# Modulation parts of a two-layer trunk: other places in the program, and another way of ordering them

## The chip, the cores and the metric

The kernel runs on one core of one Trainium2 chip. The metric is the device time of one execution in microseconds (us), median of the runs. Engines are named as in the profile: PE is TensorE's matmul row, PEld its weight loads, DVE VectorE, ACT ScalarE, POOL GpSimd, SP SyncE; a name with q (ACTq, SPq) is that engine's sequencer, here issuing DMAs.

## What is computed

One inference step of a trunk with two layers, for 512 latent tokens and 128 context tokens (640 columns together), model width 1024, all float32:

```python
def trunk_layer(x, cond, l, P, rope, ctx):
    mod = (jax.nn.silu(cond) @ P['w_mod'][l] + P['b_mod'][l])[:, None, :]
    sh1, sc1, g1, sh2, sc2, g2 = jnp.split(mod, 6, axis=-1)
    h = rmsnorm(x) * (1.0 + sc1) + sh1
    mix, ctx_out = token_mixer(h, l, P, rope, ctx)
    x = x + g1 * mix
    h = rmsnorm(x) * (1.0 + sc2) + sh2
    u = dwconv3(h @ P['w_up'][l], P['ffn_conv_w'][l], P['ffn_conv_b'][l])
    x = x + g2 * ((jax.nn.silu(u[..., :D_FF]) * u[..., D_FF:]) @ P['w_down'][l])
    return x, ctx_out
```

`token_mixer` projects h once and feeds three branches (spatial gating, a two-directional mLSTM, differential attention); each is projected by `w_branch`, multiplied by a sigmoid gate, summed, and multiplied by `w_out`. The condition vectors do not depend on the layer's input, so a layer's modulation can be computed at any time before its first use.

## The kernel before

Features lie on the 128 partitions, tokens along the free axis. A product in full precision is three passes (high x high, high x low, low x high), two matmuls of 320 columns each, so a tile of 128 outputs from 1024 inputs is 48 matmuls, and a branch tile from 512 inputs 24. These are called bulk products here: all go through `mm` (L132) or `tm` (L160). `weights` loads 512 KB through SP's queue into `raw` (3 buffers), ACT casts it to `whi`, DVE or POOL subtracts to `wlo`, 512 columns at a time (4 buffers of each).

Order of a layer: `spatial`, `mlstm_in`, four times (`mlstm_qk`, `mlstm_head`, two tiles of the first branch), `attn_v`, four times (`attn_qk`, `attn_head`, with `mlstm_out` and the second branch between them), five gates ahead, `attn_out`, the last branch over eight tiles m, `w_out`, `ffn`. The FFN runs in three groups: up products f, then down products m over the eight output tiles. The instructions are traced in program order, and a planner with a time model of its own sets the final order on every engine at build time: a ready instruction with the earlier place goes first, heads have high priority, and an instruction under `keep_in_program_order` stays behind the one traced before it on its engine.

The modulation of a layer is 12 parts (six sections of 1024, two halves of 512 each). A part needs eight DMAs of 256 KB from `w_mod`, eight float32 products of 32 x 512 (L279; the trace has 16 matmuls for them), a copy out of PSUM (`modev`, L284), four transposes (L292) and two small DVE operations (L296, L300 or L302). Sections 0 and 1 of layer 0 are made in `start`. All others are 512 wide: `mod_load` loads a part, `mod_turn` closes the open part (transposes), sums the part that was loaded, and loads the next through ACT's queue; `mod_step` does one part at once. A part occupies a PSUM tile of the tag "ms" (two buffers, also used by the heads) from its products to its close.

In the kernel before, layer 0 makes six parts and layer 1 five from `mod_step` to the last branch: one in the buffers "y", one loaded ahead into "wk", then one turn behind each tile m of the last branch, all with the same eight "wk" buffers. The FFN of layer 0 makes seven more (the rest of its own and the first five of layer 1), that of layer 1 two. With `pin` the products and the transposes keep program order.

Of the kernel before, what the change touches and what calls it, by code (L numbers as in the profile page):

```python
# [51 lines left out]

T_MLQ, T_MLG, T_SGU, T_DAQ, T_MLO, T_GATE = 0, 8, 9, 13, 21, 25
G_SG, G_ML, G_DA = 2, 1, 0


class Tags:
# [9 lines left out]
class Trunk:  # L67
    def __init__(self, nc, tc, ins, outs, depth):
        self.nc, self.tc, self.I, self.O, self.L = nc, tc, ins, outs, depth
        self.n = 0  # L70
        self.flip = 0

        self.mod_held = self.mod_open = None
        self.behind = False

    def t(self, pool, shape, dt, tag, bufs=None):
        self.n += 1
# [42 lines left out]
    def mm(self, acc, w, k0, xs, halves=(0, 1), ks=None, pin=False):  # L120

        nc = self.nc
        last = len(xs) - 1
        for k in range(len(xs)) if ks is None else ks:
            hi, lo = w[(k0 + k) // 4]
            sl = slice((k0 + k) % 4 * P, ((k0 + k) % 4 + 1) * P)
            xh, xl = xs[k]
            terms = ((hi, xh), (hi, xl), (lo, xh))
            for i, (a, b) in enumerate(terms):
                for s in halves:  # L130
                    s = slice(s * NHALF, (s + 1) * NHALF)
                    ins = nc.tensor.matmul(acc[:, s], a[:, sl], b[:, s], start=k == 0 and i == 0,  # L132
                                           stop=k == last and i == 2)
                    if pin or self.behind:
                        self.tc.keep_in_program_order(ins)
                        self.behind = False

    def fm(self, l, tile_idx, xs):
        acc = self.psA()
# [1 line left out]
        self.mm(acc, w, 0, xs)  # L141
        return acc

    def tm(self, l, kind, xs, evac):


        nc = self.nc
        for nh in range(2):
            ps = [self.t(self.ps, [P, 1024], F32, "acc", 2), self.psM()]
            accs = [ps[b // 4][:, b % 4 * 256 : b % 4 * 256 + 256] for b in range(NB)]  # L150
            for kh in range(2):
                for i, (hi, lo) in enumerate(self.weights(self.I["w_in_v"][l, kind, nh, kh], 4 * 256)):
                    for b in range(NB):
                        bs = slice(b * P, (b + 1) * P)
                        for k in range(2):
                            xh, xl = xs[4 * kh + 2 * i + k]
                            sl = slice(k * 256, (k + 1) * 256)
                            for j, (a, w) in enumerate(((xh, hi), (xh, lo), (xl, hi))):
                                first, last = kh + i + k + j == 0, kh + i + k + j == 5
                                nc.tensor.matmul(accs[b], a[:, bs], w[:, sl], start=first and b % 2 == 0,  # L160
                                                 stop=last and (b % 2 == 1 or b == NB - 1))
            for b in range(NB):
                evac(b, nh, accs[b])

# [82 lines left out]
        self.lam = self.t(lp, [P, 1], F32, "lam", 2)  # L247
        nc.vector.tensor_scalar(self.lam, s[:, 0:1], s[:, 1:2], self.lam_init, ALU.subtract, ALU.add)

    def mod_part(self, l, sec, c0, width, src, pin=False):  # L250

        self.mod_vector(*self.mod_products(l, sec, c0, width, src, pin))

    def mod_products(self, l, sec, c0, width, src, pin=False):
        return self.mod_sums(l, sec, c0, width, src, self.mod_weights(l, sec, c0, width, src), pin)

    def mod_weights(self, l, sec, c0, width, src, eng=None):
# [14 lines left out]
    def mod_sums(self, l, sec, c0, width, src, raws, pin):  # L272

        nc = self.nc
        pool, tag, per = src
        ps = self.psM()
        for k in range(KD):
            j = 32 * (k % 4)
            ins = nc.tensor.matmul(ps[j : j + 32, 0:width], self.cs[:, k, :], raws[k], start=k < 4, stop=k >= 4,  # L279
                                   tile_position=(0, j))  # L280
            if pin:
                self.tc.keep_in_program_order(ins)
        ev = self.t(pool, [P, width], F32, "ev") if width < 512 else self.t(self.sp, [P, width], F32, "modev", 1)
        (nc.scalar.copy if pin else nc.vector.tensor_copy)(ev, ps[:, 0:width])  # L284
        return l, sec, c0, width, ps, ev, pin

    def mod_vector(self, l, sec, c0, width, ps, ev, pin):
# [13 lines left out]
        else:  # L301
            nc.vector.tensor_add(m, m, b)  # L302

    def mod_step(self, src, pin=False):
        if self.mod_todo:
            l, sec, n = self.mod_todo.pop(0)
            self.mod_part(l, sec, 512 * n, 512, src, pin)

    def mod_load(self, src, eng=None):

        if self.mod_todo:
# [4 lines left out]
    def mod_turn(self, src):  # L316

        self.mod_close()
        if self.mod_held:
            self.mod_open = self.mod_sums(*self.mod_held, True)  # L320
            self.mod_held = None
            self.behind = True

        self.mod_load(src, self.nc.scalar)

# [469 lines left out]
        return ys  # L795


    def attn_v(self, l, h):
# [10 lines left out]
        self.tm(l, 2, h, evac)  # L809
        return v  # L810

    def attn_qk(self, l, h, head):

        nc, p = self.nc, self.p1
        qk = []
        for i in range(2):
            acc = self.fm(l, T_DAQ + H * i + head, h)
            x = self.t(p, [P, NT], F32, "qk")
            nc.scalar.copy(x, acc)
# [102 lines left out]
    def branch(self, l, n, h, ys, merged, ms, first=False, last=False, ahead=None):  # L922
# [4 lines left out]
        for m in ms:  # L927
# [9 lines left out]
                nc.gpsimd.tensor_add(merged[m], merged[m], th)  # L937
            if last:
                out.append(self.split(merged[m], self.hp, "h", scale=0.5))
                self.mod_turn((p, "wk", 1))  # L940
        if last:
            self.mod_close()
        return out


    def ffn(self, l, h, accs, x, p2, nxt):
# [28 lines left out]
        for f0, f1 in FFN_PARTS:  # L975

            for f in range(len(acts), min(f1 + 1, NF)):
                up(f)
                if f in (2, 4):
                    self.mod_turn((p2, "mw", 1))  # L980
            g2 = self.mods[l, 5]
            down = lambda m: self.I["w_down"][l, m, :, f0 * P : f1 * P]
# [16 lines left out]
    def run(self):  # L999
# [3 lines left out]
        with ExitStack() as ctx:  # L1003
# [15 lines left out]
            for l in range(self.L):  # L1019
# [4 lines left out]
                self.layer_consts(l)  # L1024
                with tc.tile_pool(name=f"p1{l}", bufs=1, reuse_waits="tile") as p1:
                    self.p1 = Tags(p1, {"wk": 8, "tg": 2, "st": 6, "qk": 4, "v": 1, "y": 8, "hs": 5, "mg": 8})
                    merged = [self.t(self.p1, [P, NT], F32, "mg") for _ in range(KD)]
                    self.mod_todo = [(l, s, n) for s in (2, 3, 4) for n in range(2)][1 if l else 0 :]
                    ys = self.spatial(l, h, accs)
                    v, rows = self.mlstm_in(l, h)  # L1030
                    sums = self.t(self.sp, [P, H, NB], F32, "mlsum", 1)
                    hs = []
                    for i in range(H):
                        q, k = self.mlstm_qk(l, h, i)
                        if i == 0:
                            rows = (*rows[:2], self.gate_columns(rows[2]))
                        with tc.high_priority():
                            hs.append(self.mlstm_head(l, i, q, k, v, rows, sums))
                        self.branch(l, G_SG, h, ys, merged, (2 * i, 2 * i + 1), first=True)
                    self.lambdas(l)  # L1040
                    v = self.attn_v(l, h)
                    dsums = self.t(self.sp, [P, H, NB], F32, "dasum", 1)
                    os = []
                    for i in range(H):
                        q, k = self.attn_qk(l, h, i)
                        with tc.high_priority():
                            os.append(self.attn_head(l, i, q, k, v, dsums))
                        if i == 0:
                            ys = self.mlstm_out(l, h, hs, sums)
                        else:  # L1050
                            self.branch(l, G_ML, h, ys, merged, range(*FILL_ML[i - 1 : i + 1]))
                    ahead = {m: self.gate(l, G_DA, m, h, t) for m, t in enumerate(AHEAD)}
                    self.mod_step((self.p1, "y", 1), pin=True)
                    self.mod_load((self.p1, "wk", 1))
                    ys = self.attn_out(os, dsums)
                    mix = self.branch(l, G_DA, h, ys, merged, range(KD), last=True, ahead=ahead)
                with tc.tile_pool(name=f"p2{l}", bufs=1, reuse_waits="tile") as p2:
# [12 lines left out]
                    h2, accs = self.handoff([I["w_out"][l, m] for m in (KD - 2, KD - 1)], mix, x, self.mods[l, 2], st,  # L1070
                                            [I["w_up"][l, i] for i in range(2)])
                    nxt = l + 1 < self.L
                    self.mod_todo = [(l, 5, 0), (l, 5, 1)]
                    if nxt:
                        self.mod_todo += [(l + 1, s, n) for s in (0, 1) for n in range(2)] + [(l + 1, 2, 0)]
                    h, accs = self.ffn(l, h2, accs, x, tags, nxt)
                    if nxt:
                        for k in range(KD):
# [104 lines left out]
```

## Time and profile before

| | |
|---|---|
| median of 3 runs | 2437.73 us (2436.23 to 2439.9) |
| profiled execution, its time | 2434.44 us |
| its span in the profile | 2432.6 us |
| PE busy, PEld busy | 2391.6 us (98%), 2314.6 us (95%) |
| DVE, ACT, POOL busy | 1137.4, 949.9, 668.5 us |
| granted TensorE clock, mean | 0.997 |
| DMA | 227.39 MB, mean 93 GB/s |

The span runs from the first to the last instruction; the execution's own time has 1.8 us around it. The end of a matmul is modelled in these records, and matmuls overlap, so a stretch with a busy PE may still hold waits: the start-to-start distance of the products and the PEld column show them.

### The profile page before, as it was taken

What the parts mean: (1) busy time and instruction counts of PE and PEld (TensorE: products, weight loads), DVE (VectorE), ACT (ScalarE), POOL (GpSimd) and SP (SyncE); (2) the same over time, 40 slices, a digit from 0 to 9 for tenths busy, and PEclk for the clock granted to TensorE, in tenths of its full rate; (3) what the DMA queues carried; (4) which work ended last, traced back from release to release, by engine and by line L of the source; (5) the groups of instructions that cost most, each with busy time, mean ns of one, the idle gap of its engine ahead of it and who ended that gap; (6) DMA issues with size and microseconds to landing.
All of it is one profiled execution on the core that took longest, in us unless ns stands there. A gap on an engine that the chain in (4) does not pass through costs nothing.

```text
span 2432.6 us, 40611 instructions
## 1 busy us (share of the span) xinstructions
PE 2391.6 (98%) x16708; PEld 2314.6 (95%) x16708; DVE 1137.4 (47%) x2102; ACT 949.9 (39%) x1737; POOL 668.5 (27%) x486
## 2 busy tenths in 40 slices
PE   8999999999999999999999999999999999999998
PEld 7999999999699999999999999999987999999998
DVE  5455546554246423424446455455533454343344
ACT  4433335545145323323454332454542443232334
POOL 2312232332222322323213222323322223232231
PEclk9999999999999999999999999999999999999999
DMA  7222221124541444222322212211233432222222
GB/s 278 70 79 66 66 78 54 63 76 135 170 151 64 137 138 139 73 75 79 97 87 70 72 64 68 71 58 63 83 126 123 148 104 66 83 70 79 79 70 70
DMA packets 88761, 227.39 MB, mean 93 GB/s; under 512 B 9472, under 2 KB 23936, under 8 KB 88576
## 3 DMA queue, kind: packets, MB, share of 16 engines
q1 hardware_dynamic: 72448, 195.43, 24.5%
q10 hardware_dynamic: 16128, 29.37, 3.6%
q8 instruction: 131, 2.15, 0.4%
q14 instruction: 54, 0.44, 0.1%
HBM read 217.41 MB, written 7.35 MB: 92 GB/s over the span
## 4 chain that ended last, share of the span: by engine, by line
PE 93%; DVE 3%; DMA 2%; ACT 1%; issue 1%; ACTq 0%; SPq 0%; DVEq 0%; POOL 0%; POOLq 0%
PE acc L132 76%; PE acc L160 6%; PE ms L906 2%; PE ms L877 2%; PE ms L279 2%; PE ms L160 1%; DMA wk<-w_mod 1%; PE ms L899 1%; PE ms L753 1%; PE ms L742 1%; PE ms L755 1%; DVE h L393 1%; DVE x L476 0%; DVE wlo L104 0%; PE ms L707 0%
## 5 line engine op out<-in xcount | busy, mean ns | idle before, releaser
L132 PE MATMUL acc<-h,whi 128*128 128x320 f32 x6464 | 1243.5, 310 | 9.8 <-DVE h L393 5.0
L132 PEld LDWEIGHTS acc<-h,whi 128*128 128x128 f32 x6464 | 1019.2, 188 | 21.5 <-DVE h L393 9.3
L103 ACT CAST whi<-raw 128x512 fp32r<-128x512 f32 x596 | 365.2, 614 | 998.4 <-PE acc L132 725.9
L132 PE MATMUL acc<-h,wlo 128*128 128x320 f32 x3232 | 754.9, 309 | 0.0
L104 POOL TENSOR_TENSOR wlo<-raw,whi 128x512 fp32r<-128x512 f32 (+1 forms) x298 | 390.8, 1312 | 1320.4 <-ACT whi L103 1299.3
L132 PEld LDWEIGHTS acc<-h,wlo 128*128 128x128 f32 x3232 | 544.2, 188 | 0.2
L104 DVE TENSOR_TENSOR wlo<-raw,whi 128x512 fp32r<-128x512 f32 (+1 forms) x298 | 240.4, 807 | 457.8 <-ACT whi L103 438.0
L132 PE MATMUL acc<-act,whi 128*128 128x320 f32 x1408 | 268.9, 310 | 0.0
L132 PEld LDWEIGHTS acc<-act,whi 128*128 128x128 f32 x1408 | 221.9, 188 | 3.4 <-issue 3.4
L132 PE MATMUL acc<-act,wlo 128*128 128x320 f32 x704 | 165.6, 309 | 0.0
L536 DVE SCALAR_TENSOR_TENSOR x<-acc,mod,x 128x128 f32<-128x128 f32 (+3 forms) x136 | 66.3, 526 | 193.9 <-PE acc L132 193.9
L132 PE MATMUL acc<-y,whi 128*128 128x320 f32 x768 | 151.5, 312 | 1.7 <-DVE y L117 1.7
L160 PE MATMUL acc<-whi,h 128*128 128x256 f32 x768 | 145.7, 283 | 0.0
L169 DVE SCALAR_TENSOR_TENSOR cw<-acc,vec,cw 128x511 f32<-128x511 f32 (+1 forms) x176 | 95.7, 544 | 105.1 <-ACT cw L167 103.7
L132 PEld LDWEIGHTS acc<-y,whi 128*128 128x128 f32 x768 | 121.0, 188 | 8.9 <-issue 5.0
L160 PEld LDWEIGHTS acc<-whi,h 128*128 128x128 f32 x768 | 123.0, 192 | 0.0
L132 PEld LDWEIGHTS acc<-act,wlo 128*128 128x128 f32 x704 | 119.0, 188 | 0.0
L954 POOL TENSOR_TENSOR cw<-cw,cw 128x640 f32<-128x640 f32 x44 | 69.4, 1576 | 156.4 <-DVE cw L171 152.9
L160 PE MATMUL acc<-wlo,h 128*128 128x256 f32 x384 | 108.7, 283 | 0.0
L171 DVE SCALAR_TENSOR_TENSOR cw<-acc,vec,cw 128x511 f32<-128x511 f32 (+1 forms) x176 | 96.7, 550 | 6.1
L132 PE MATMUL acc<-y,wlo 128*128 128x320 f32 x384 | 90.6, 313 | 0.0
L885 ACT ACTIVATE wk<-ms,mx 128x640 f32<-128x640 f32 (+1 forms) x80 | 56.7, 709 | 76.6 <-DVE mx L883 73.1
(256 smaller groups left out, 2418.6 us busy)
## 6 DMA issues: line engine op xcount, KB each, us to landing
raw<-w_in_f SPq DMA_DIRECT2D x98, 512.0 KB, 3.3
raw<-w_up SPq DMA_DIRECT2D x88, 512.0 KB, 3.3
wk<-w_mod ACTq DMA_DIRECT2D x56, 256.0 KB, 5.1
mw<-w_mod ACTq DMA_DIRECT2D x56, 256.0 KB, 5.4
raw<-w_down SPq DMA_DIRECT2D x32, 448.0 KB, 3.3
raw<-w_in_v SPq DMA_DIRECT2D x24, 512.0 KB, 3.5
raw<-w_branch SPq DMA_DIRECT2D x24, 512.0 KB, 3.4
mw<-w_mod SPq DMA_DIRECT2D x16, 512.0 KB, 8.7
```

The costliest lines, as they stand in the source:

```text
L103: nc.scalar.copy(hi, raw[:, a:b])
L104: self.alt().tensor_sub(lo, raw[:, a:b], hi.bitcast(F32))
L132: ins = nc.tensor.matmul(acc[:, s], a[:, sl], b[:, s], start=k == 0 and i == 0, stop=k == last and i == 2)
L160: nc.tensor.matmul(accs[b], a[:, bs], w[:, sl], start=first and b % 2 == 0, stop=last and (b % 2 == 1 or b == NB - 1))
L169: nc.vector.scalar_tensor_tensor(dst[:, a + 1 : b], acc[:, a : b - 1], w0, dst[:, a + 1 : b], ALU.mult, ALU.add)
L171: nc.vector.scalar_tensor_tensor(dst[:, a : b - 1], acc[:, a + 1 : b], w2, dst[:, a : b - 1], ALU.mult, ALU.add)
L279: ins = nc.tensor.matmul(ps[j : j + 32, 0:width], self.cs[:, k, :], raws[k], start=k < 4, stop=k >= 4, tile_position=(0, j))
L536: self.nc.vector.scalar_tensor_tensor(x[:, a:b], acc[:, a:b], g[:, k, i : i + 1], x[:, a:b], ALU.mult, ALU.add)
L877: nc.tensor.matmul(ps[:, s : s + 320], st[:, qs], kk[:, s : s + 320], start=i == 0, stop=i == 1)
L885: nc.scalar.activation(e[:, 0:nk], ps[:, 0:nk], AF.Exp, bias=mx, scale=scale, accum_out=sm[:, j : j + 1])
L906: nc.tensor.matmul(po, at[:, c * P : (c + 1) * P], vv, start=c == 0, stop=c == n - 1)
L954: nc.gpsimd.tensor_mul(cs[0], cs[0], cs[1])
```

## The change

Four things. (1) The parts made around the last branch are gone: `mod_step`, the load into "wk" and the turns in `branch`. (2) Layer 0 makes its six parts earlier in the mixers: three in the buffers "mg" (the sums of the branches, not yet allocated then), after `spatial`, after `mlstm_in` and after the first `mlstm_qk`; three in the buffers "y" between the first branch's end and the use of the same tag by `mlstm_out`: in the middle of `attn_v`, after it, and between the two products of the first `attn_qk`. (3) Layer 1 makes none: the FFN of layer 0 makes 14 parts (its own last two and all twelve of layer 1), with a turn at every even f in place of 2 and 4; the FFN of layer 1 has none left. (4) A part is no longer pinned: its first product is ordered behind the last bulk matmul traced, each product behind the one before, and the next bulk matmul behind the last product; these are orders on PE's queue and no waits. The transposes are free for the planner. The copy out of PSUM is always on ACT.

```diff
@@ class Trunk
-        self.behind = False
+        self.behind = self.bulk = None
@@ mm
-                    if pin or self.behind:
-                        self.tc.keep_in_program_order(ins)
-                        self.behind = False
+                    self.queue(ins, pin)
+
+    def after(self, ins, prev):
+        self.tc.add_manual_dep(ins.ins, prev.ins.name, ORDER, reason="queued in this order")
+
+    def queue(self, ins, pin=False):
+        if pin:
+            self.tc.keep_in_program_order(ins)
+        if self.behind:
+            self.after(ins, self.behind)
+            self.behind = None
+        self.bulk = ins
@@ tm
+            if nh and between:
+                between()
@@ mod_sums
             if pin:
                 self.tc.keep_in_program_order(ins)
+            elif k:
+                self.after(ins, prev)
+            elif self.bulk:
+                self.after(ins, self.bulk)
+            prev = ins
+        if not pin:
+            self.behind = ins
@@ mod_turn
-            self.mod_open = self.mod_sums(*self.mod_held, True)
+            self.mod_open = self.mod_sums(*self.mod_held, False)
             self.mod_held = None
-            self.behind = True
@@ attn_qk
         for i in range(2):
+            if i and turn:
+                self.mod_turn(None)
             acc = self.fm(l, T_DAQ + H * i + head, h)
@@ branch
-                self.mod_turn((p, "wk", 1))
-        if last:
-            self.mod_close()
@@ ffn
-                if f in (2, 4):
+                if f % 2 == 0:
                     self.mod_turn((p2, "mw", 1))
@@ run
-                    merged = [self.t(self.p1, [P, NT], F32, "mg") for _ in range(KD)]
-                    self.mod_todo = [(l, s, n) for s in (2, 3, 4) for n in range(2)][1 if l else 0 :]
+                    self.mod_todo = [] if l else [(l, s, n) for s in (2, 3, 4) for n in range(2)]
+                    room = (self.p1, "mg", 1)
+                    self.mod_load(room)
                     ys = self.spatial(l, h, accs)
+                    self.mod_turn(room)
                     v, rows = self.mlstm_in(l, h)
+                    self.mod_turn(room)
...
                         if i == 0:
+                            todo, self.mod_todo = self.mod_todo, []
+                            self.mod_turn(None)
+                            self.mod_todo = todo
+                            merged = [self.t(self.p1, [P, NT], F32, "mg") for _ in range(KD)]
                             rows = (*rows[:2], self.gate_columns(rows[2]))
...
+                        self.mod_close()
+                    room = (self.p1, "y", 1)
+                    self.mod_load(room)
                     self.lambdas(l)
-                    v = self.attn_v(l, h)
+                    v = self.attn_v(l, h, lambda: self.mod_turn(room))
+                    self.mod_turn(room)
...
                         if i == 0:
+                            self.mod_close()
                             ys = self.mlstm_out(l, h, hs, sums)
...
-                    self.mod_step((self.p1, "y", 1), pin=True)
-                    self.mod_load((self.p1, "wk", 1))
...
-                    self.mod_todo = [(l, 5, 0), (l, 5, 1)]
                     if nxt:
-                        self.mod_todo += [(l + 1, s, n) for s in (0, 1) for n in range(2)] + [(l + 1, 2, 0)]
+                        self.mod_todo = [(l, 5, 0), (l, 5, 1)] + [(l + 1, s, n) for s in range(6) for n in range(2)]
```

## Rows read from the trace of the kernel before

**Rows 1.** The page: span, busy time of each engine, chain's shares by engine.

```profile
span 2432.6 us, 40611 instructions
PE 2391.6 (98%) x16708; PEld 2314.6 (95%) x16708; DVE 1137.4 (47%) x2102; ACT 949.9 (39%) x1737; POOL 668.5 (27%) x486
PE 93%; DVE 3%; DMA 2%; ACT 1%; issue 1%; ACTq 0%; SPq 0%; DVEq 0%; POOL 0%; POOLq 0%
```

**Rows 2.** Windows: stretch, busy per engine (instructions), PE clock, DMA share, GB/s.

```profile
135.00:311.00 176.00, 176.00 (x1259) 175.61 (x1258) 89.70 (x169) 54.35 (x86) 41.26 (x31) 1.00 0.21 67
606.00:655.00 49.00, 45.84 (x221) 24.44 (x221) 13.41 (x17) 6.67 (x11) 11.37 (x8) 1.00 0.58 193
1810.00:1853.00 43.00, 39.81 (x206) 23.60 (x206) 11.88 (x16) 6.24 (x10) 9.05 (x7) 1.00 0.51 171
883.00:898.00 15.00, 15.00 (x112) 13.19 (x104) 3.38 (x10) 2.85 (x5) 2.60 (x2) 1.00 0.63 202
```

**Rows 3.** Waits of PE's weight loads: waiter, releaser, total us, times, longest.

```profile
PEld ms L279 <- DMA wk<-w_mod: 32.0, 45, 2.1
```

**Rows 4.** Chain of waits, layer 0's last branch: start us, us, what.

```profile
591.73 8.21 PE acc L132 x56
599.93 1.98 PE ms L279 x16
...
606.86 3.79 PE acc L132 x24
...
654.47 10.76 PE acc L132 x72
665.23 0.44 PE ms L292 x4
```

**Rows 5.** Chain of waits, layer 1's last branch.

```profile
1803.96 1.98 PE ms L279 x16
...
1810.88 3.78 PE acc L132 x24
...
1852.08 0.44 PE ms L292 x4
```

**Rows 6.** Chain of waits in the mixers of layer 0.

```profile
135.19 14.09 PE acc L132 x96
...
341.72 17.62 PE acc L132 x120
```

**Rows 7.** Chain of waits in the FFN of layer 0.

```profile
765.77 28.39 PE acc L132 x192
794.16 1.85 PE ms L279 x16
...
883.71 12.52 PE acc L132 x84
...
926.27 1.98 PE ms L279 x16
...
928.97 0.66 PE ms L292 x4
```

**Rows 8.** Timeline of ACT in layer 0's last branch: start, us, engine, line, operation.

```profile
623.17 0.59 ACT L284 COPY modev<-ms 128x512 f32<-128x512 f32 x1 [5.38 <-PE ms L279]
623.25 3.71 ACTq L265 DMA_DIRECT2D wk<-w_mod  x8
...
633.72 0.59 ACT L284 COPY modev<-ms 128x512 f32<-128x512 f32 x1 [6.04 <-PE ms L279]
```

**Rows 9.** Timeline of all engines where the first mixer begins.

```profile
40.68 10.77 SPq L97 DMA_DIRECT2D raw<-w_in_v  x4
...
48.30 1.12 ACT L103 CAST whi<-raw 128x512 fp32r<-128x512 f32 x2
...
51.85 0.28 PE L160 MATMUL ms<-whi,h 128*128 128x256 f32 x1
```

**Rows 10.** Timeline of DVE in the first mLSTM head.

```profile
162.91 0.82 DVE L722 TENSOR_TENSOR st<-ms,wk 128x640 f32<-128x640 f32 x1
```

More of the change, by code (lines that the diff above doesn't have):

```diff
@@ L54 @@
 G_SG, G_ML, G_DA = 2, 1, 0
+ORDER = mybir.DependencyInfo(mybir.DependencyClass.NoSync, mybir.DependencyReason.DATA)
 class Tags:
@@ L142, in fm, with tm @@
         return acc
-    def tm(self, l, kind, xs, evac):
+    def tm(self, l, kind, xs, evac, between=None):
         nc = self.nc
         for nh in range(2):
+            if nh and between:
+                between()
             ps = [self.t(self.ps, [P, 1024], F32, "acc", 2), self.psM()]
@@ L159, in tm @@
                                 first, last = kh + i + k + j == 0, kh + i + k + j == 5
-                                nc.tensor.matmul(accs[b], a[:, bs], w[:, sl], start=first and b % 2 == 0,
-                                                 stop=last and (b % 2 == 1 or b == NB - 1))
+                                self.queue(nc.tensor.matmul(accs[b], a[:, bs], w[:, sl], start=first and b % 2 == 0,
+                                                            stop=last and (b % 2 == 1 or b == NB - 1)))
             for b in range(NB):
@@ L248, in lambdas @@
         nc.vector.tensor_scalar(self.lam, s[:, 0:1], s[:, 1:2], self.lam_init, ALU.subtract, ALU.add)
-    def mod_part(self, l, sec, c0, width, src, pin=False):
-        self.mod_vector(*self.mod_products(l, sec, c0, width, src, pin))
     def mod_products(self, l, sec, c0, width, src, pin=False):
@@ L282, in mod_sums @@
                 self.tc.keep_in_program_order(ins)
+            elif k:
[5 more added lines that the diff above has]
+            self.behind = ins
         ev = self.t(pool, [P, width], F32, "ev") if width < 512 else self.t(self.sp, [P, width], F32, "modev", 1)
-        (nc.scalar.copy if pin else nc.vector.tensor_copy)(ev, ps[:, 0:width])
+        nc.scalar.copy(ev, ps[:, 0:width])
         return l, sec, c0, width, ps, ev, pin
@@ L302, in mod_vector @@
             nc.vector.tensor_add(m, m, b)
[L304 to L307, printed above, removed]
     def mod_load(self, src, eng=None):
@@ L795, in mlstm_out, with attn_v @@
         return ys
-    def attn_v(self, l, h):
+    def attn_v(self, l, h, turn):
         nc, p = self.nc, self.p1
@@ L807, in evac, with attn_qk @@
                 nc.sync.dma_start(self.O["nv"][l, :, nh * 256 : (nh + 1) * 256], v[b][:, nh * 256 : (nh + 1) * 256])
-        self.tm(l, 2, h, evac)
+        self.tm(l, 2, h, evac, turn)
         return v
-    def attn_qk(self, l, h, head):
+    def attn_qk(self, l, h, head, turn):
         nc, p = self.nc, self.p1
@@ L1044, in run @@
                     for i in range(H):
-                        q, k = self.attn_qk(l, h, i)
+                        q, k = self.attn_qk(l, h, i, i == 0)
                         with tc.high_priority():
```

## The prediction

> **What bounds the kernel now.** I read the page first: PE is busy for 98% of the span, its weight loads for 95%, and 93% of the chain that ended last is PE [rows 1]. So a change that keeps the number of products, as this one does, can gain only where PE stands still. The busy share hides such places, because the end of a matmul is modelled; the PEld column of the windows shows them. In the mixers it fills the stretch (175.61 of 176 us), in the last branch of either layer it fills about half (24.44 of 49 us, 23.60 of 43 us) [rows 2]. The waits name the cause: PE's weight loads wait 32.0 us for w_mod transfers, in 45 pieces [rows 3]. The chain of waits places them: between the gates ahead and the sixth tile of the last branch, the five tiles' products are torn apart [rows 4, 5]. The timeline of ACT gives the mechanism. A part's copy begins at 623.17, its eight DMAs of the next part are issued over 3.71 us, and the copy of that next part begins only at 633.72 [rows 8]: a turn takes 10.55 us, because all turns use the same eight buffers, while the tile between two turns has 24 products, 24 x 0.147 = 3.5 us. The pitch of 0.147 us is 17.62 / 120 [rows 6].
>
> **What a part costs where nothing is late.** In the FFN, bulk products run up to 794.16, the part's 16 matmuls take 1.85 us, and bulk goes on at once [rows 7]; the four transposes cost 0.44 us [rows 4]. So 2.29 us, all of it on the path.
>
> **Removed from layer 0's last branch.** The stretch from 599.93 to 654.47 is 54.54 us, and one set of transposes follows at 665.23 with 0.44 us [rows 4]. What must remain: from the last product before `attn_out` to the first branch product, 606.86 - 601.91 = 4.95 us (head transposes, splits on ACT and DVE; the y splits wait for PSUM and not for the part, so I leave this as it is), and 5 x 24 x 0.147 = 17.6 us, together 22.6. Removed: 54.54 - 22.6 + 0.44 = **32.4 us** for six parts. The next limit there would be the weights: one 1024-column tile per two tiles m, 7.0 us, the rate at which the other stages keep PE full [rows 2].
>
> **Removed from layer 1's last branch.** 1803.96 to 1852.52 (the end of the transposes) is 48.56 us, what remains is again 4.94 + 17.6 [rows 5], removed **26.0 us** for five parts. **Removed from layer 1's FFN:** two parts, 2 x 2.29 = **4.6 us**. **Unpinned transposes:** at the end of the first down group the close follows its part directly, so PE waits for the copy: products end at 928.25, transposes at 929.63, 1.38 us in place of 0.44 [rows 7]. Free to move, they save **0.9 us**.
>
> **Added to layer 0's FFN.** Seven parts, 7 x 2.29 = **16.0 us**. Are their loads late? The gaps between turns are 28.4 us (192 products) in the up groups and 12.5 us plus 2.3 us in the down groups [rows 7], against the 10.55 us of a load turn [rows 8]; the down groups carry such turns already, at 202 GB/s, without a gap in the chain [rows 2, 7]. What hides the loads is that bulk; where only 24 products lie between turns it is gone, and a part costs 10.55 - 3.5 - 2.3 = 4.7 us more. On ACT the casts of later weights queue behind the copy and the eight issues; they have four `whi` buffers, 4 x 3.5 us of products, ahead of them, and the block is about 4.3 us [rows 8].
>
> **Added to layer 0's mixers.** Six parts, 6 x 2.29 = **13.7 us**. Three doubts, each bounded.
> The gaps are a whole stage or half of `attn_v` for four of the parts, 14.09 us for the third (two tiles of `mlstm_qk`), and for the sixth only one `attn_qk` tile, 48 x 0.147 = 7.05 us [rows 6]. There a turn of 7.05 + 0.44 + 1.85 = 9.34 us meets a load of 10.55: **1.2 us** late; bounds 0 (other work moves in) and 4.7 as above.
> The first load enters SP's queue ahead of `w_in_v`, whose four issues start at 40.68, whose first cast is at 48.30 and whose first product at 51.85 [rows 9]. A load of eight DMAs costs at most some 3.7 us of issue plus its transfer, 2.1 MB at about 200 GB/s or more, 10 us; of that 7 us or so lie in the slack between issue and cast. No row shows which buffers are free when. Bounds 0 and 7, and I take **1.5 us**, near the lower end, since PE there waits for h in any case.
> From the third part to its close one of the two "ms" buffers is taken, while the first mLSTM head needs some nine of them in turn. Each turn loses its overlap with an evacuation of 0.82 us [rows 10], 7 to 9 us for the head; PE has two gates, two branch tiles and the next `mlstm_qk` to fill it, and it was full before [rows 2]. Bounds 0 and 9, I take 0. After the sixth part the transposes come ahead of the head's first product, so nothing is held there.
>
> **A rule against the change.** The Trainium skill, "DMA: Bandwidth & Descriptors", section "Queues, rings and completion order", says that ACT's and SP's DMAs share the same 16 engines, which alternate between the two queues; so a part loaded beside weights may get half the rate. With the page's 358 GB/s, half for 2.1 MB is an estimate of 11.7 us; the late sixth part would then cost about 3 us in place of 1.2 and the total would be about 2 us higher. The trace fits sharing (both queues together moved 193 GB/s in the last branch [rows 2]) but shows 10.55 us.
>
> **The sum.** -32.4 - 26.0 - 4.6 - 0.9 + 16.0 + 13.7 + 1.2 + 1.5 = -31.5 us. The profiled execution took 2434.44 us with a span of 2432.6, so it would become 2402.9. It lies 3.3 us under the median of the runs, so on the median's scale 2437.73 - 31.5 = **2406 us**. What is late next: nothing single; the waits left are at the hand-offs between normalisation and products, and PE is full elsewhere.
>
> **Rivals.**
> A, the new places are partly late. The mixers' 14 us gap has only 3.5 us to spare, ACT must issue the load at once there, and the held PSUM buffer and the first load come together: 4.7 + 9 + 5.5 us above what I took make 2406 + 19 = 2425 at worst, 2416 in the middle. For it: the order is fixed at build time by a time model. Against: PE full in the mixers with bulk to spare [rows 2].
> B, slower. Because bulk products are now ordered behind a part's products, a late part stops all bulk. If the 13 moved parts were each late as in the last branch now, 13 x 4.7 = 61 us, the time would be 2406 + 61 - 1 = 2466. It decides where the load turn outgrows the gap; it passes zero gain when the mean wait is over 33 / 13 = 2.5 us, that is when turns of 14.8 us are overrun by that much. Against: these very turns run now without waiting [rows 7].
> C, no difference: the change doesn't do what it says, because under the w_mod waits lies another limit of the last branch (weights, splits) which keeps its length, so that the parts only change place. Then the last branch stays near 49 us in both layers and the time is about 2437. Against: without the parts the five tiles need three weight tiles, 1.6 MB in 17.6 us, half the rate now seen there [rows 2].
>
> **How the numbers follow.** My forecast (2402 to 2410) has 0.70, A 0.18, B 0.05, C 0.07. A and the forecast are faster by more than 0.2%, about what a measurement of this kernel can tell from no change: 0.88 faster, 0.07 the same, 0.05 slower. The range takes the bounds of the unknown costs: low end with the two late terms at zero and 2 us of scatter, 2401; high end that of A, 2425. It leaves out B and C.
>
> **What would show it.** Right: in both last branches PEld fills the stretch, 22.6 us from the end of the gates ahead to the sixth tile; no wait for w_mod over 3 us in total; in the FFN 14 parts of 1.85 + 0.44 us with bulk directly behind; the mixers of layer 0 longer by 15 us, those of layer 1 up to the last branch unchanged. Wrong: a PEld wait for w_mod in the mixers, products at the first mixer's begin after 53.5, PEld under 95% in 135 to 311 us, or a last branch well over 23 us.

## The result and the profile after

| | before | after |
|---|---|---|
| median of the runs | 2438.48 us | 2408.80 us (2406.03 to 2410.14) |
| ratio, 95% interval | | 0.9878, 0.9861 to 0.9895 |
| profiled execution, its time | 2434.44 us | 2406.03 us |
| its span | 2432.6 us | 2404.2 us |
| granted TensorE clock, mean | 0.997 | 0.996 |

The change is faster by 1.2%. The forecast, 2406 us, lies 2.8 us under the median; the spans of the two profiled executions differ by 28.4 us where the sum said 31.5.

The page of the kernel after, which answers [rows 1]: the span, the busy time of each engine, the shares of the chain that ended last.

```profile
span 2404.2 us, 40627 instructions
PE 2369.4 (99%) x16708; PEld 2314.0 (96%) x16708; DVE 1129.8 (47%) x2102; ACT 950.2 (40%) x1737; POOL 670.4 (28%) x486
PE 95%; DVE 3%; ACT 1%; issue 0%; DMA 0%; SPq 0%; DVEq 0%; ACTq 0%; POOL 0%; POOLq 0%
```

The number of matmuls is the same and the weight loads' busy time is the same (2314.6 and 2314.0 us); what fell is the time around them. In the chain, DMA had 2% of the chain and has 0%.

Windows of the kernel after over the stretches of [rows 2]: stretch, busy time and instructions of PE, PEld, DVE, ACT, POOL, granted clock, DMA share, GB/s.

```profile
135.00:311.00 176.00, 175.72 (x1258) 172.05 (x1257) 89.00 (x165) 53.99 (x87) 41.36 (x31) 1.00 0.24 80
606.00:655.00 49.00, 46.59 (x321) 45.70 (x320) 16.51 (x20) 15.44 (x24) 22.49 (x15) 1.00 0.21 71
1810.00:1853.00 43.00, 42.29 (x288) 42.29 (x289) 12.37 (x16) 11.08 (x18) 19.73 (x13) 1.00 0.18 62
```

In the second and third row PEld has gone from 24.44 to 45.70 us and from 23.60 to 42.29 us, and the DMA rate from 193 to 71 and from 171 to 62 GB/s. The mixers, in the first row, have their parts in them now and lose 3.6 us of PEld.

Waits of PE's weight loads in the kernel after, two of the rows of a part's products: waiter, releaser, total us, times, longest. The second answers [rows 3], 32.0 us; the first, time in which nothing that the profile shows is waited for, was 11.1 us in 45 pieces before.

```profile
PEld ms L290 <- issue: 15.5, 60, 0.3
...
PEld ms L290 <- DMA y<-w_mod: 1.3, 3, 0.6
```

The chain of the kernel after at the three places: the last branch of layer 0 (answers [rows 4]), the sixth part in layer 0's mixers (answers [rows 6]), a down group of layer 0's FFN (answers [rows 7]). L133 is a bulk product, L290 a part's product, L310 a transpose.

```profile
608.50 7.93 PE acc L133 x54
...
616.45 0.62 ACT whi L104
617.07 0.60 ACT hs L933
617.67 0.69 ACT y L117
...
621.90 38.12 PE acc L133 x258
```

```profile
351.22 0.43 PE ms L310 x4
...
351.68 1.92 PE ms L290 x16
353.60 7.24 PE acc L133 x48
360.84 0.43 PE ms L310 x4
361.27 3.37 PE ms L290 x16
364.64 7.24 PE acc L133 x48
```

```profile
1022.31 1.85 PE ms L290 x16
1024.16 12.51 PE acc L133 x84
1036.67 0.44 PE ms L310 x4
1037.11 1.85 PE ms L290 x16
1038.96 12.51 PE acc L133 x84
```

The last branch is one piece of 258 products. In the second fence one part is late: 3.37 us in place of 1.85. In the third the period is 14.80 us for 84 products; by the pitch of [rows 6] they are 84 x 0.1468 = 12.33 us, so a part in a place without waiting costs **2.47 us**, not 2.29.

To see where the rest went I set the start of each of the 14400 bulk products of the kernel after against the product of the same number in the kernel before. The difference changes for good only where something was added or removed, and at the hand-offs (the normalisation between two stages):

| stretch | change, us |
|---|---|
| up to the first mixer | -0.35 |
| mixers of layer 0, six parts | +17.1 |
| last branch of layer 0 | -32.1 |
| hand-off to the FFN of layer 0 | +0.4 |
| FFN of layer 0, seven parts more | +16.5 |
| last branch of layer 1 | -25.5 |
| hand-off to the FFN of layer 1 | +1.1 |
| FFN of layer 1, two parts less | -5.0 |
| sum | -27.8 |

The other 0.6 us of the spans' 28.4 lie behind the last bulk product.

### The profile page after: what moved, and what is told of

Its sections match the earlier page's. It is cut to its first block, busy times and chain, and to the rows that moved or that the text cites. A ratio compares the mean times of both kernels' runs of the same rounds, so it can differ in the third digit from the quotient of the medians.

```text
span 2404.2 us, 40627 instructions
## 1 busy us (share of the span) xinstructions
PE 2369.4 (99%) x16708; PEld 2314.0 (96%) x16708; DVE 1129.8 (47%) x2102; ACT 950.2 (40%) x1737; POOL 670.4 (28%) x486
## 4 chain that ended last, share of the span: by engine, by line
PE 95%; DVE 3%; ACT 1%; issue 0%; DMA 0%; SPq 0%; DVEq 0%; ACTq 0%; POOL 0%; POOLq 0%
PE acc L133 78%; PE acc L174 6%; PE ms L290 2%; PE ms L920 2%; PE ms L891 2%; PE ms L174 1%; PE ms L913 1%; PE ms L765 1%; PE ms L754 1%; PE ms L767 1%; DVE x L488 0%; PE ms L719 0%; PE ms L585 0%; PE ms L310 0%; DVE h L405 0%
## 5 line engine op out<-in xcount | busy, mean ns | idle before, releaser
L133 PE MATMUL acc<-h,whi 128*128 128x320 f32 x6464 | 1247.1, 311 | 8.9 <-DVE h L405 5.1
L133 PEld LDWEIGHTS acc<-h,whi 128*128 128x128 f32 x6464 | 1021.0, 188 | 26.4 <-DVE h L405 9.1
L133 PE MATMUL acc<-h,wlo 128*128 128x320 f32 x3232 | 757.8, 310 | 0.0
L104 ACT CAST whi<-raw 128x512 fp32r<-128x512 f32 x596 | 365.1, 614 | 993.4 <-PE acc L133 724.5
L133 PEld LDWEIGHTS acc<-h,wlo 128*128 128x128 f32 x3232 | 545.6, 188 | 0.1
L133 PE MATMUL acc<-act,whi 128*128 128x320 f32 x1408 | 269.3, 310 | 0.0
L133 PEld LDWEIGHTS acc<-act,whi 128*128 128x128 f32 x1408 | 221.9, 188 | 5.9 <-issue 5.9
L133 PE MATMUL acc<-act,wlo 128*128 128x320 f32 x704 | 165.8, 310 | 0.0
L133 PE MATMUL acc<-y,whi 128*128 128x320 f32 x768 | 150.7, 312 | 1.4 <-DVE y L118 1.4
L133 PEld LDWEIGHTS acc<-y,whi 128*128 128x128 f32 x768 | 121.4, 188 | 2.0 <-DVE y L118 1.9
L133 PEld LDWEIGHTS acc<-act,wlo 128*128 128x128 f32 x704 | 119.0, 188 | 0.0
L133 PE MATMUL acc<-y,wlo 128*128 128x320 f32 x384 | 90.2, 313 | 0.0
```

What stands on the lines that cost most here:

```text
L104: nc.scalar.copy(hi, raw[:, a:b])
```

## The experiments

"Bulk time" below is this same comparison.

**One layer alone, from either side.** The kernel before with only layer 1's parts moved:

```diff
-                if f in (2, 4):
+                if f % 2 == 0:
                     self.mod_turn((p2, "mw", 1))
...
-                    self.mod_todo = [(l, s, n) for s in (2, 3, 4) for n in range(2)][1 if l else 0 :]
+                    self.mod_todo = [] if l else [(l, s, n) for s in (2, 3, 4) for n in range(2)]
...
-                        self.mod_todo += [(l + 1, s, n) for s in (0, 1) for n in range(2)] + [(l + 1, 2, 0)]
+                        self.mod_todo = [(l, 5, 0), (l, 5, 1)] + [(l + 1, s, n) for s in range(6) for n in range(2)]
```

> The kernel before, with only layer 1's seven parts (five around its last branch, two of its FFN) moved to the FFN of layer 0; pinned as before, layer 0's mixers as before. Theory P (the gain is the place: no wait for a load): -25.5 us (layer 1's last branch) -5.0 (its FFN) +7 x 2.48 (FFN of layer 0) = -13 us, about 2425 us. Rival O (the gain is the freer order on PE, which is not changed here): within 3 us of 2438.

Measured: 2425.0 us, ratio 0.9949 (0.9934 to 0.9964). In bulk time the FFN of layer 0 took 17.4 us more, 7 x 2.49, the last branch of layer 1 25.5 less, the FFN of layer 1 5.0 less. And the kernel after with layer 0's six parts put back, ordered as in the kernel after but not pinned:

```diff
+                self.mod_turn((p, "wk", 1))
...
+                    self.mod_load((self.p1, "y", 1))
...
+                    self.mod_turn(None)
+                    self.mod_close()
...
+                    self.mod_load((self.p1, "wk", 1))
                     ys = self.attn_out(os, dsums)
```

> The kernel after, with only layer 0's six parts back around its last branch (one in the y buffers, five in the wk buffers); ordered behind single bulk products as in the kernel after. P: the last branch again 54 us, +32, the mixers without the parts, -17, together +15 us, about 2424 us, with waits for w_mod of about 18 us in that branch. O: other work moves into the waits, since nothing is pinned: within 5 us of 2409.

Measured: 2425.61 us, ratio 0.9952 (0.9935 to 0.997). Waits of PE's weight loads in this kernel:

```profile
PEld ms L290 <- DMA wk<-w_mod: 18.0, 26, 1.9
```

So the two layers' shares add up: layer 1's is 2438.18 (the kernel before in this comparison) - 2425.0 = 13.2 us, layer 0's 2425.61 - 2408.80 = 16.8 us, together 30.0 for the 29.7 of the whole change. And the waits come back with the place, though nothing is pinned. The new ordering is not what removed them.

**The buffers alone.** The kernel before with its parts where they were, but loaded in turn into two sets of eight buffers, so that a load starts one turn earlier:

```diff
+            r = self.t(pool, [P, per, width], F32, ("st" if k < 6 else "qk") if tag == "two" else tag)
...
+        if self.mod_next:
+            self.mod_held = self.mod_next.pop(0)
+            if self.mod_todo:
+                l, sec, n = self.mod_todo.pop(0)
+                part = (l, sec, 512 * n, 512, (src[0], self.sets[0], 1))
+                self.mod_next.append((*part, self.mod_weights(*part, self.nc.scalar)))
+                self.sets.reverse()
+            return
```

> The kernel before with every part where it was, but two sets of eight buffers taken in turn at the last branch (wk; six of st and two of qk), so that a load has two tiles' time. P in its narrow form (a turn is as long as its load because all turns share one set): a load turn of 10.55 us against 2 x (3.5 + 2.48) = 12.0 us, so no wait: layer 0 -17 us, layer 1 -13.6 us, about 2408 us, like the kernel after. Rival W (the transfers themselves bound the stage: a part and its share of the weights, 2.36 MB, at the 193 GB/s seen there take 12 us): no gain, 2438 us. Between them if the rate rises only part of the way.

Measured: 2407.55 us, ratio 0.9876 (0.9861 to 0.989). The chain of this kernel in layer 0's last branch (L280 products, L293 transposes of a part), and its window of 613 to 655 us:

```profile
618.19 1.85 PE ms L280 x16
620.05 3.72 PE acc L133 x24
623.76 0.44 PE ms L293 x4
624.20 1.85 PE ms L280 x16
626.05 3.72 PE acc L133 x24
```

```profile
613.00:655.00 42.00, 42.00 (x299) 34.13 (x292) 13.92 (x20) 8.29 (x14) 15.08 (x11) 1.00 0.59 201
```

A turn takes 624.20 - 618.19 = 6.0 us where it took 10.55, and a gain of the same size (0.9876 and 0.9878) needed no other place. This settles the cause of the old waits: one set of buffers, free only when its own products had ended, and not the rate of the DMA engines. It also speaks against rival C of the prediction: no other limit of the last branch showed. The Trainium skill, "DMA: Bandwidth & Descriptors", section "Queues, rings and completion order", says that the two queues' DMAs alternate on the same 16 engines. This trace does not contradict it, but 201 GB/s from both queues together kept PE fed here, so that the half rate which the prediction feared did not bind.

**A load turn has its own length.** The kernel after with a turn behind every down tile, which leaves 42 products between turns:

```diff
-                elif m % 2:
+                else:
                     self.mod_turn((p2, "mw", 1))
```

> The kernel after, but in the FFN's first two groups a part is turned behind every down tile in place of every second one, so that eight turns stand in a row with 42 products between them. The load turn measured in the last branch of the kernel before is 10.55 us; a turn here has 42 products, 6.25 us (half of the 12.51 us for 84 in the kernel after), and 2.3 us of the part. Theory G (a load turn with one set of buffers has its own length, and a part is late by what the gap lacks): each of the seven turns behind the first is 10.55 - 8.55 = 2.0 us late, with 11.0 us in place of 10.55 it is 2.4 us; the weight loads of PE wait for w_mod there and the time is 13 to 17 us above the kernel after, 2422 to 2426 us. Rival F (the loads were slow only in the last branch, because ACT and the queues are busier there; in the FFN they keep up): no wait, 2408 to 2410 us.

Measured: 2423.72 us, ratio 0.9941 (0.992 to 0.9963), so theory G. The chain of this kernel in the first down group, and the wait behind it:

```profile
915.56 0.43 PE ms L310 x4
915.99 3.63 PE ms L290 x16
919.62 6.35 PE acc L133 x42
925.97 0.44 PE ms L310 x4
926.41 3.44 PE ms L290 x16
```

```profile
PEld ms L290 <- DMA mw<-w_mod: 15.3, 29, 1.8
```

This turn is 925.97 - 915.56 = 10.41 us, as the 10.55 of [rows 8], in another stage and with 42 products between in place of 24; the seven turns of this group take 10.2 to 11.8 us. The products of a part take 3.4 to 3.6 us here in place of 1.85: the part waits for what the gap lacks. So the gap decides: with the 12.51 us of bulk between turns that the kernel after has here nothing waits, with 6.35 every part behind the first does.

**The late sixth part.** The kernel after with this part one tile later:

```diff
         for i in range(2):
+            acc = self.fm(l, T_DAQ + H * i + head, h)
             if i and turn:
                 self.mod_turn(None)
-            acc = self.fm(l, T_DAQ + H * i + head, h)
```

> The kernel after, with layer 0's sixth part behind both products of the first attn_qk in place of between them, so that its load has 14.1 us in place of 7.05. Theory P (a part is late by load turn minus gap): the 1.9 us of this part go, about 2407 us, its 16 matmuls take 1.9 us in place of 3.4. Rival (the wait is a queue of ACT's or a shortage of transfers at that place): they stay.

Measured: 2403.68 us, ratio 0.9869 (0.9852 to 0.9885); bulk time at this place -2.8 us, more than the lateness. (The medians differ by more, 2408.80 - 2403.68 = 5.1 us, but they come from two comparisons and their intervals overlap.) The windows of 372 to 400 us, where the first attention head runs, of the kernel after and of this one:

```profile
372.00:400.00 28.00, 26.57 (x185) 25.74 (x184) 19.55 (x42) 17.17 (x35) 7.69 (x6) 1.00 0.19 60
```

```profile
372.00:400.00 28.00, 28.00 (x198) 27.53 (x199) 19.87 (x43) 19.14 (x38) 5.89 (x5) 1.00 0.16 50
```

In the kernel after PE stands still for 1.4 us there (26.57 of 28), in this one not at all. The lateness of 1.5 us (3.37 - 1.85 above) and these 1.4 us are the 2.8. The part did not bring the second wait: most of it is one matmul of the head that waits for DVE, and the kernel before, without the part, has it too. That matmul in the kernel before and in the kernel after, with the idle time ahead of it in brackets:

```profile
365.75 0.82 PE L877 MATMUL ms<-st,st 128*128 128x320 f32 x4 [1.13 <-DVE st L844]
```

```profile
381.86 0.82 PE L891 MATMUL ms<-st,st 128*128 128x320 f32 x4 [1.05 <-DVE st L858]
```

So the later place removed the part's own wait and filled one that was there already. Whether the part itself fills it or the order that the planner then found, I did not isolate.

**Parts into a wait.** The kernel after with one part of each layer taken out of other work and put inside `attn_out`, where PE waits for ACT and DVE:

```diff
+                    self.mod_todo = [(l, 5 if l else 4, 1)]
+                    self.mod_load((self.p1, "wk", 1))
                     ys = self.attn_out(os, dsums)
+                    self.mod_turn(None)
+                    self.mod_close()
```

> The kernel after, with layer 0's sixth part, and one of layer 1's parts from the FFN of layer 0, summed inside attn_out from the wk buffers, loaded ahead, free of any pin: PE idles there some 2.9 us in each layer (5.48 us between the last gate ahead and the first branch product, less four sets of transposes of 0.65). Theory P: the late 1.9 us go, and each of the two parts costs between 0 and 2.5 us in place of 2.48: 2402 to 2407 us. Rival: the copy on ACT delays the splits of y, and the part costs what it cost: 2407 us or more.

Measured: 2404.06 us, ratio 0.9869 (0.9854 to 0.9883). Its chain at the end of layer 0's mixers:

```profile
612.69 0.55 PE acc L793 x5
613.24 1.98 PE ms L290 x16
...
615.24 0.59 ACT modev L302
...
618.57 21.50 PE acc L133 x145
```

The part's products run behind the first head transposes (L793) and ahead of the first branch product; the bulk moves by 0.65 us for it, not by 2.48. In the chain the part stands ahead of the y splits, which wait for its copy on ACT.

The kernel before had the first part of each layer close to this place, pinned ahead of the head transposes. From the end of the last gate to the first branch product it takes 606.86 - 599.93 = 6.93 us [rows 4], the kernel after 621.90 - 616.42 = 5.48. So this part cost 1.45 us there, in either layer, and the change took it to places where a part costs 2.48.

The last kernel on this question has both places.

> The kernel after with the two cheaper places together: layer 0's sixth part behind both products of the first attn_qk, and one part inside attn_out in either layer (layer 0 its own FFN's first part, layer 1 its last), each taken out of the FFN of layer 0. Theory P (a part costs nothing where PE would wait anyway): by the product times of the two kernels that tried the places apart, -2.85 us for the sixth part and 0.65 - 2.48 = -1.8 us for each of the other two, -6.5 us against the kernel after: 2408.8 - 6.5 = 2402.3 us, ratio to the kernel before about 0.985. Rival Q (the covers are one and the same wait, or the part in front of the first head takes what attn_out would have waited for): 2404 to 2407 us.

```diff
+            acc = self.fm(l, T_DAQ + H * i + head, h)
             if i and turn:
                 self.mod_turn(None)
-            acc = self.fm(l, T_DAQ + H * i + head, h)
...
+                    self.mod_todo = [(l, 5, 1 if l else 0)]
+                    self.mod_load((self.p1, "wk", 1))
                     ys = self.attn_out(os, dsums)
+                    self.mod_turn(None)
+                    self.mod_close()
```

Both edits together, with two parts less in layer 0's FFN. Measured: 2400.34 us, ratio 0.9853 (0.9835 to 0.987). Bulk time, against the kernel after: -2.7 at the sixth part, +0.64 and +0.65 in the two `attn_out`, -5.0 in the FFN, together -6.4; the spans differ by 2404.2 - 2398.0 = 6.2. Its ratio is the lowest of the study, 0.25% under that of the kernel after, but the two intervals overlap (0.9861 to 0.987): that it is faster is shown by the bulk time of one execution of each, and not by the medians.

**What the pin does.** The kernel after with products and transposes kept in program order:

```diff
-        if not pin:
+        if width == 512:
             self.behind = ins
...
-            self.mod_open = self.mod_sums(*self.mod_held, False)
+            self.mod_open = self.mod_sums(*self.mod_held, True)
```

> The kernel after with products and transposes of the parts pinned to program order, as in the kernel before. P: only the close at the end of the FFN's first down group waits again, +0.9 us, and up to 2 us more in the mixers, 2409 to 2412 us. O: a good part of the 29 us is gone, 2420 us or more.

Measured: 2427.38 us, ratio 0.9957 (0.9942 to 0.9972): my theory P missed by 15 us. The records say where. The transposes of the sixth part, which come at 371.72 us in the kernel after, stand in this kernel at:

```profile
L310 PE MATMUL ms<-ident,modev x4: 272/272/273, 469.9 to 470.3; 128*128 128x128 f32 x4
```

That part's products ended at 365.4, so for 105 us the heads had one "ms" buffer in place of two. Bulk products went ahead in their place: by 482 us they were 9.2 us early against the kernel after. They were then missing at the end of the mixers, where the heads still ran. The window of 600 to 643 us of this kernel, a wait in it, and the same window of the kernel after:

```profile
600.00:643.00 43.00, 31.40 (x170) 28.09 (x169) 19.70 (x38) 20.93 (x44) 4.99 (x3) 0.80 0.09 31
```

```profile
PEld ms L920 <- ACT wk L915: 5.1, 4, 2.1
```

```profile
600.00:643.00 43.00, 40.59 (x284) 39.69 (x284) 15.63 (x20) 14.85 (x25) 18.98 (x12) 1.00 0.21 68
```

PE does 170 matmuls there in place of 284, waiting above all for ACT, at a granted clock of 0.80. The bulk falls back by 28.5 us, and 20 stay; how much of that is the lower clock was not separated. Two kernels test this reading. The first closes the sixth part ahead of the head and keeps the pin:

```diff
                         q, k = self.attn_qk(l, h, i, i == 0)
+                        self.mod_close()
                         with tc.high_priority():
                             os.append(self.attn_head(l, i, q, k, v, dsums))
```

> Everything pinned as in the run of the pinned kernel (2427 us), with one thing changed: the sixth part is closed ahead of the first attention head in place of behind it, so that its PSUM buffer is free while the head runs. Theory H (the pin cost 18.6 us because the buffer was held over that head): 2408 to 2411 us, PE full from 600 us to the gates ahead. Rival (the pin of the products itself costs): 2420 us or more.

Measured: 2409.11 us, ratio 0.989 (0.9875 to 0.9905), with 284 matmuls in 600 to 643 us again. The pin as such costs nothing; the late close did. In this pair the held buffer and the late place of the pinned transposes go together; the second kernel holds the buffer without a pin. It takes the kernel after and holds the third part over all four mLSTM heads:

```diff
                         self.branch(l, G_SG, h, ys, merged, (2 * i, 2 * i + 1), first=True)
-                        self.mod_close()
+                    self.mod_close()
```

> The kernel after, with the third part closed behind all four mLSTM heads in place of behind the first, so that one of the two ms buffers is held by a finished part while all four heads run. Theory B (bulk products cover it, as the prediction took it): within 2 us of 2409. Theory H (a head with one buffer runs later and bulk runs ahead of it, and the time is paid where bulk runs out): 7 to 9 us for each of three further heads, less what the 28.8 us of bulk in attn_v cover: 0 to +27 us, seen at the end of the heads and not where the buffer is held.

Measured: 2414.73 us, ratio 0.9911 (0.9897 to 0.9926). Bulk time: 9.2 us early by 317, then 14.1 us lost at once, where no bulk product runs beside the last head from 322 to 336 us; 5 us remain. The window of 316 to 332 us of this kernel, and the same of the kernel after, which has bulk there:

```profile
316.00:332.00 16.00, 13.49 (x103) 12.24 (x102) 9.67 (x19) 4.16 (x6) 4.32 (x3) 1.00 0.00 1
```

```profile
316.00:332.00 16.00, 16.00 (x139) 16.00 (x138) 8.01 (x19) 4.62 (x7) 3.88 (x3) 1.00 0.61 190
```

So a held buffer alone does this: the bulk runs ahead, and the time is lost where it has run out. Another 2 to 3 us of the profiled execution came at the hand-off to layer 0's FFN, and the last experiment turns to such places.

**The clock at the hand-offs.** Two kernels unchanged, one more profiled execution of each:

> The kernel after unchanged, one more profiled execution. Theory C (the granted clock falls at one hand-off or another by chance of the execution): the windows of 4 us at the three hand-offs show other clocks than in the first profile of the same kernel (1.00 at 725 to 737 us, 0.60 at 1922 to 1926 us) and the span moves by 1 to 3 us with them. Rival S (it belongs to the kernel's order of work): the same clocks at the same places.

> The kernel with two parts inside attn_out unchanged, one more profiled execution. Theory C (chance of the execution): the windows at 725 to 737, 1236 to 1244 and 1919 to 1927 us show other clocks than before in this kernel (0.56 to 0.79), and the time comes nearer to 2402 us, what the product times alone give (2408.8 - 5.2 = 2403.6 and less). Rival S (the order of work): the same falls at the same places, and about 2404 us again.

Measured: 2406.49 us and 2400.49 us (one execution each). Windows of the kernel after at the two hand-offs where the executions differ most, the first execution and then the second:

```profile
1240.00:1244.00 4.00, 3.60 (x24) 3.31 (x25) 4.00 (x11) 2.36 (x7) 0.00 (x0) 1.00 0.61 213
...
1922.00:1926.00 4.00, 4.00 (x20) 3.97 (x21) 3.30 (x9) 1.98 (x5) 0.00 (x0) 0.60 0.45 131
```

```profile
1240.00:1244.00 4.00, 3.96 (x18) 3.93 (x19) 3.19 (x8) 1.98 (x5) 0.00 (x0) 0.60 0.35 131
...
1922.00:1926.00 4.00, 3.59 (x25) 3.30 (x26) 4.00 (x11) 2.24 (x7) 0.00 (x0) 1.00 0.39 131
```

The fall has changed places within one kernel; bulk time moves with it, +1.5 us at 1240 and -1.6 at 1926. In the kernel with parts in `attn_out` the window of 733 to 737 us went from 0.56 to 1.00, -3.0 us. So the same program has the fall at other places in another execution (theory C), worth 1.5 to 3 us at a place. Both hand-off terms of the table above go with it: against the first execution, the second moves by -0.6 us at 750 and by -1.2 over the hand-off at 1926, back at the kernel before, with +1.5 at 1240 instead. It has another +1.5 at 1811 us, inside layer 1's `attn_out`, where the granted clock of 1810 to 1815 us is 0.66 in place of 1.00; so the fall is not bound to the hand-offs, and the second execution was no shorter than the first. The traced execution of the kernel before has no such fall between its first and its last 25 us. Its other executions do vary: the 27 beside the experiments take from 2432.91 us at a mean granted clock of 0.997 to 2441.72 us at 0.993.

## Why the prediction was right, point by point

**What bounded the kernel.** Right. The PEld column and the w_mod waits named the stretches; PEld is busy for 45.70 of 49 us and 42.29 of 43 there now, and the single buffer set was the cause (two sets alone gave 0.9876).

**Removed.** Layer 0's last branch 32.1 us for 32.4, layer 1's 25.5 for 26.0, layer 1's FFN 5.0 for 4.6, the unpinned close 0.9 for 0.9. The two last branches fell short by what I set for `attn_out`: from 616.42 to 621.90 it takes 5.48 us, not 4.95. I had read the y splits as waiting for PSUM and not for the part, and left that stretch as it was. In the chain of the kernel before they wait behind the part's copy:

```profile
601.93 0.58 ACT modev L284
...
602.52 0.80 ACT y L116
```

In the kernel after a cast (L104, 0.62 us) and the evacuation `hs` (L933, 0.60 us) stand there in its place; before, both ran beside the part's products. So of the 1.98 us of products that I counted as removed there, only 1.45 were.

**The price of a part: the mis-sized term.** 2.29 us was the part's own instructions; 2.48 is what the bulk moves by. The 0.2 us lie in the bulk piece behind the part and were in the rows: 84 products of [rows 7] take 12.52 us, and 84 x 0.1468 is 12.33. I counted the part and took the bulk at its pitch, without comparing the two. With 13 parts added and two removed it is 11 x 0.19 = 2.1 us, the largest piece of the miss. The start times of the records place half of it: the second bulk product behind a part starts 0.25 us after the first, where the pitch is 0.147. Why it does, no run here shows.

**The three doubts.** The late sixth part: 3.37 - 1.85 = 1.5 us for 1.2. A wait for w_mod in the mixers was also one of the signs that I named for being wrong; the 1.3 us of it are this part, which the sum already had as late. The first load: the first product of `w_in_v` is at 51.50 us for 51.85 before, so 0 and not 1.5. The held PSUM buffer: 0 in this kernel, as I took, within some 0.4 us, and for the reason given, since PE had bulk to put there: at the first head the bulk runs 4.9 us ahead and falls back by as much. But the bound of 9 us was not the right bound: held over an attention head it cost 20 us, by another way than the one I counted (the lost overlap of each turn), namely bulk work used up early and missing later. 0.7 us more in the mixers stay unplaced.

**Not in the sum:** the hand-offs, +1.6 us together, the granted clock of these two executions by the last experiment.

**The rivals.** A did not come: the kernel after has no w_mod wait for the parts with 14 us gaps or for the first load, and the late 1.5 us are the sixth part, a term of the forecast's own sum. B's mechanism exists, as the turns behind every tile show, about 2 us per part where the gap is 8.6 us; the kernel's gaps are longer everywhere but at the sixth part. C fell with the result, since both last branches lost most of what the parts cost them. The estimate worked out from the Trainium skill, "DMA: Bandwidth & Descriptors", section "Queues, rings and completion order", was 11.7 us for a load and about 3 us late (by the working of the sixth part, 11.7 - 9.34 = 2.4). It was too dark: the turn at this part measured 364.64 - 353.60 = 11.04 us, its products included, and the part was 1.5 us late.

The terms that were too low (2.1 for the parts, 0.8 for the last branches, 1.6 for the hand-offs, 1.0 in the mixers: 5.5) and those too high (1.5 for the first load, 0.35 ahead of the mixers: 1.85) differ by 3.7 us: from -31.5 to -27.8. That errors of both signs stand in the sum, and that the medians lie only 2.8 us from the forecast, is in part luck; the mechanism, and the size of each large term, is not.

## What to carry to other kernels

Price a moved piece by how far the regular work behind it shifts, not by the sum of its own instructions. A prefetch with one set of buffers has a turn of its own length, here 10 to 12 us; either the gap between turns is longer, or there are two sets, which here gave the same gain without moving the work. Before a piece is moved, look at what ran beside it: a part that this change took out of a wait had cost 1.45 us there. A buffer held while others need it may cost nothing where it is held and much later, when the work that filled its place has run out; and the best place for a small piece is a wait of the engine, where 2.48 us became 0.65.

## What the runs showed of the hardware beyond this

At the hand-offs between `w_out`, the FFN and the next layer PE has waits for normalisation (2.85 of 4 us busy in 729 to 733 us of the kernel after, 1.86 of 3 in 1919 to 1922), and in some executions the granted clock is lower for the 4 to 8 us at or behind them: 0.56 to 0.8 in such windows of 4 us, a mixture of the two levels, and in the kernel that held the third part the lower one alone, 1.2 GHz:

```profile
741.00:745.00 4.00, 4.00 (x18) 4.00 (x18) 1.58 (x5) 1.02 (x3) 0.00 (x0) 0.50 0.08 34
```

(A window of that kernel with the columns as above: 18 matmuls in place of some 28.) The same program had it at 1922 us in one execution and at 1240 us in another, with 1.00 at the other place, and it cost 1.5 to 3 us of time each time. I had expected a given program to repeat this. The second execution had it at 1811 us too, behind the waits inside `attn_out` (PE busy for 2.59 of the 5 us before). A comparison of single executions below 0.1% should look at these windows first.
